# Stage one of a decoder trunk on one Trainium2 core: two weight blocks on each arriving x, another order of transfers, sums and factors at other steps

## The chip, the core and the metric

The kernel runs on one core of one Trainium2 chip. A core has TensorE (matrix products; PE in the profile, with PEld for the loading of its weights), VectorE (DVE), ScalarE (ACT), GpSimd (POOL) and the queue engine SyncE (SP), which here only issues transfers. Products go into PSUM, and everything else lives in SBUF. The metric is the device time of one execution in microseconds, the median over the runs shown.

## The reference, cut to what matters

One layer of a hybrid decoder, T = 1024 tokens and 1024 channels in fp32. The normed input is multiplied by `w_in`, and its columns go to three groups of heads; then come `w_out`, a gated MLP and a gate.

```python
z = rmsnorm(h, norm_mix_g[l]) @ w_in[l]
a_q, a_f, a_i, a_g, b_q, b_k, b_v, c_in = jnp.split(z, splits, axis=-1)
o_a = hgrn2_mix(a_q, a_f, a_i, a_g, ...)
o_b = dilated_window_mix(b_q, b_k, b_v)
o_c, v_first = rwkv7_mix(c_in, ...)
h = h + jnp.concatenate([o_a, o_b, o_c], axis=-1) @ w_out[l]
h = h + conv_glu_ffn(rmsnorm(h, norm_ffn_g[l]), ffn_up[l], ...)
h = h + jax.nn.sigmoid(rmsnorm(h, norm_ple_g[l]) @ ple_gate[l]) * (p[l] @ ple_proj[l])
...
# in rwkv7_mix: a mix of each column with that of the token before
cm = cf + (c_prev - cf) * mu
r, k, v, wd, ad, gd = jnp.split(cm, splits, axis=-1)
w = -jax.nn.softplus(-(w0 + jnp.tanh(wd) @ w2)) - 0.5
a = jax.nn.sigmoid(a0 + ad @ a2)
kk = k * k_k, divided by its norm in each head
state = state * decay + (state @ -kk) (kk a)^T + v k^T      # token by token
```

The factor of the norm, 1 / sqrt(mean(x^2) + eps), is one number for each token.

## The kernel before

x is held transposed: channels on the 128 partitions in 8 tiles k = 0 to 7, tokens along the row in two halves of 512 (HT). A block of `w_in` is 1024 x 128, with index j, brought as one tile of 128 x 1024 (`wraw`) with its 8 pieces side by side. An fp32 product is made of three products of rounded parts (`mm3`, L130, L132, L134): high x by high weight (`whi`), low x (`xl`) by high weight, high x (`xh`) by low weight (`wlo`). For each half of a block (pieces 0 to 3, and 4 to 7) `split2` makes whi by a copy on ACT (L106), and wlo by a subtraction on DVE or POOL (L108). `split_w` chooses the engine by whether a running number is odd; that number counts every tile that gets a name, so it depends on how many were named before.

**Stage one** is `mix_norm` (from L336). The products don't wait for the norm: x is multiplied by its gain g and split into xh (ACT, L378) and xl (DVE, L379), and the factor, called R or rstd, is multiplied in afterwards, on the result. Three blocks of `w_in` are worked on here: j = 0 (in the program later `lora`, the columns wd and ad), j = 1 (`sg`, the column gd) in the pool dps of two PSUM buffers `dp`, and j = 2 (`k`) in `dp2`, which lies in a PSUM pool ps0 that is closed later. Its place then goes to the pool `mx`, from which the small product `lo` (L610) and others take theirs. For the factor, `square` sums x^2 over the tiles (ACT, and the additions on DVE into `acc`); `factor_sums` multiplies by ones on TensorE (L167), scales on DVE (L173) and takes the power on POOL (L175); `factor` spreads the result on TensorE (L181, with the identity in `cst`) and copies it on ACT into R (L395). `idle_products` are products of a constant tile whose result nothing reads (`pwarm`).

The queue of SP brings, in this order: 238 columns of the parameters `par` (119 KB), the halves of w0, x by pairs of tiles, w1, w2, the second half of x, and the constants `cst`; the first two tiles of x come over ACT's queue, the last 512 columns of `par` over POOL's.

**Behind stage one** `rwkv` begins. `mix_in` scales a result with R (`scale`, L308), multiplies by 1 - mu on ACT (L547) and adds mu times the result of the token before on DVE (L548). `rwkv_prep` then makes, from lora, the products `lo` and their sigmoids (`a`, `w`, L611), two exponentials of w (L613, L614), two scans along the tokens on DVE (`gam`, `ig`, L621, each with a tile `dz` that POOL zeroes), and the number `ka`; from k the sums `kks` on TensorE (L634), their power on POOL (`kr`, L638), its widening on ACT (`krw`, L187) and its spread on TensorE (`kkb`); from all that kkn (L652), `ar`, `bhat` (L655), and the copy `bb` (L697), which the product `sc` (L714) takes. Meanwhile TensorE multiplies the blocks r, v and others.

TensorE's order is written out by hand here (`manual_schedule`), and in the first half of stage one also ACT's and DVE's; elsewhere a scheduler orders each engine's instructions by its own estimates.

## Time and profile before

| what | us |
|---|---|
| median of 3 runs (1437.71 to 1438.71) | 1437.77 |
| the profiled execution's own time | 1439.43 |
| its span | 1437.70 |
| TensorE busy | 1412.9 |
| VectorE busy | 1089.5 |
| ScalarE busy | 655.2 |
| GpSimd busy | 452.1 |

The profile shows one execution. A row of its timeline has the start, the length (over all instructions of the row where it has a count behind x), the engine, the line, the operation, what it writes and from what, and in brackets the idle time of the engine ahead of it and what ended that. A row of waits has the waiting instruction, the one that it waited for, the sum, the number and the longest. Matmuls overlap: one of 128 x 512 shows some 0.4 us, and they start 0.23 us apart.

### The profile page before, as it was taken

Reading aid. Unit: us, or ns where it says so; the run is one execution under the profiler, and the core shown is the slowest. Engines: PE = TensorE matmul, PEld = TensorE weight load, DVE = VectorE, ACT = ScalarE, POOL = GpSimd, SP = SyncE. Lnnn points to the kernel's source line nnn. Section 1 sums busy time; section 2 is a strip of 40 time slices with the busy share of each in tenths; the row PEclk is TensorE's granted clock in tenths of the full one; section 3 lists DMA queues with packets and bytes.
Section 4 is the critical chain, followed back from the end, with each engine's and each line's share of the span. In section 5 each row is a group of like instructions: output and inputs, shape, how many; then the busy total and the mean of one; then the engine's idle time right before and its main releaser. Section 6 shows DMA issues by size and latency. Waiting matters only on the chain.

```text
span 1437.7 us, 20276 instructions
## 1 busy us (share of the span) xinstructions
PE 1412.9 (98%) x7406; PEld 1167.0 (81%) x7406; DVE 1089.5 (76%) x1649; ACT 655.2 (46%) x1237; POOL 452.1 (31%) x362
## 2 busy tenths in 40 slices
PE   9999999999999999999999999999999999999997
PEld 7788887888877877788878888888888888888886
DVE  7567575674786787348898988898888799777685
ACT  7531443214535676335644334344444445455552
POOL 2322443124421241222145445454444000001343
PEclk9999999999999999999999999999999999999999
DMA  5223021240350320364423333323333983352344
GB/s 212 76 88 111 30 75 59 83 115 30 104 183 30 118 81 30 99 221 173 166 80 104 110 111 110 105 94 110 103 110 110 326 281 95 101 171 60 117 144 142
DMA packets 80019, 167.84 MB, mean 117 GB/s; under 512 B 20080, under 2 KB 22256, under 8 KB 79920
## 3 DMA queue, kind: packets, MB, share of 16 engines
q1 hardware_dynamic: 66144, 145.97, 31.0%
q10 hardware_dynamic: 12832, 17.04, 3.5%
q0 software_dynamic: 944, 3.54, 0.7%
q8 instruction: 58, 0.95, 0.3%
q14 instruction: 41, 0.34, 0.1%
HBM read 120.12 MB, written 46.40 MB: 116 GB/s over the span
## 4 chain that ended last, share of the span: by engine, by line
PE 86%; DVE 6%; ACT 3%; issue 2%; DMA 1%; POOL 1%; SPq 0%; DVEq 0%; ACTq 0%; POOLq 0%
PE bg L1414 16%; PE bv L1414 12%; PE dp L130 8%; PE dp L132 8%; PE dp L134 8%; PE bg L1732 7%; PE bv L1732 7%; PE hsc L1093 2%; PE bv L130 1%; PE bv L134 1%; PE bv L132 1%; PE swq L1249 1%; PE bg L134 1%; PE bg L130 1%; PE bg L132 1%
## 5 line engine op out<-in xcount | busy, mean ns | idle before, releaser
L130 PE MATMUL dp<-xh,whi 128*128 128x512 f32 x544 | 197.5, 408 | 0.9 <-ACT xh L378 0.8
L132 PE MATMUL dp<-xl,whi 128*128 128x512 f32 x544 | 188.7, 392 | 1.1 <-DVE xl L379 1.1
L134 PE MATMUL dp<-xh,wlo 128*128 128x512 f32 x544 | 188.2, 391 | 0.0
L108 POOL TENSOR_TENSOR wlo<-wraw,whi 128x512 fp32r<-128x512 f32 x63 | 90.4, 1439 | 243.3 <-ACT whi L106 229.3
L108 POOL TENSOR_TENSOR wlo<-raw,whi 128x512 fp32r<-128x512 f32 x84 | 136.4, 1643 | 75.3 <-ACT whi L106 75.3
L1414 PE MATMUL bg<-t,whi 128*128 128x512 f32 x352 | 132.5, 389 | 0.8 <-DVE ct L1617 0.8
L106 ACT CAST whi<-wraw 128x512 fp32r<-128x512 f32 x120 | 72.8, 617 | 120.5 <-PE dp L132 75.8
L130 PEld LDWEIGHTS dp<-xh,whi 128*128 128x128 f32 x544 | 101.8, 189 | 23.8 <-issue 3.4
L134 PEld LDWEIGHTS dp<-xh,wlo 128*128 128x128 f32 x544 | 102.3, 188 | 21.6
L132 PEld LDWEIGHTS dp<-xl,whi 128*128 128x128 f32 x544 | 102.7, 189 | 21.1 <-DVE xl L379 1.7
L108 POOL TENSOR_TENSOR wlo<-s,whi 128x512 fp32r<-128x512 f32 x44 | 66.9, 1521 | 158.2 <-ACT whi L106 155.7
L1732 PE MATMUL bg<-t,whi 128*128 128x512 f32 x308 | 95.0, 389 | 0.0
L1732 PE MATMUL bv<-t,whi 128*128 128x512 f32 x308 | 94.8, 389 | 0.0
L106 ACT CAST whi<-s 128x512 fp32r<-128x512 f32 x66 | 39.1, 621 | 120.7 <-PE bg L1414 113.2
L106 ACT CAST whi<-raw 128x512 fp32r<-128x512 f32 x88 | 52.6, 619 | 90.8 <-issue 48.5
L175 POOL TENSOR_TENSOR rst<-rst,mhalf 128x4 f32<-128x4 f32 (+1 forms) x9 | 10.3, 1140 | 221.4 <-DVE rst L173 221.4
L1414 PEld LDWEIGHTS bg<-t,whi 128*128 128x128 f32 x352 | 66.0, 188 | 14.6 <-ACT whi L106 1.1
L108 DVE TENSOR_TENSOR wlo<-wraw,whi 128x512 fp32r<-128x512 f32 x57 | 45.1, 792 | 38.2 <-ACT whi L106 33.9
L1728 ACT CAST t<-t 128x512 fp32r<-128x512 f32 x77 | 47.8, 622 | 47.5 <-PE bv L1732 33.0
L1732 PEld LDWEIGHTS bv<-t,whi 128*128 128x128 f32 x308 | 57.8, 188 | 12.0
L1732 PEld LDWEIGHTS bg<-t,whi 128*128 128x128 f32 x308 | 57.8, 188 | 12.0
L1414 PE MATMUL bg<-t,wlo 128*128 128x512 f32 x176 | 67.2, 389 | 0.0
(440 smaller groups left out, 3617.4 us busy)
## 6 DMA issues: line engine op xcount, KB each, us to landing
raw<-in_ffn_up_dram SPq DMA_DIRECT2D x44, 512.0 KB, 3.6
wraw<-in_w_in_dram SPq DMA_DIRECT2D x29, 512.0 KB, 3.9
z<-zst SPq DMA_DIRECT2D x18, 512.0 KB, 2.8
gb<-ct SPq DMA_DIRECT2D x33, 256.0 KB, 2.0
t<-gb SPq DMA_DIRECT2D x33, 256.0 KB, 2.8
t<-gt SPq DMA_DIRECT2D x33, 256.0 KB, 2.6
zl<-z SPq DMA_DIRECT2D x16, 512.0 KB, 4.9
wraw<-in_ple_gate_dram SPq DMA_DIRECT2D x16, 512.0 KB, 3.5
```

Source lines behind the costliest of these rows:

```text
L106: nc.scalar.copy(hi, src)
L108: eng.tensor_tensor(lo, src, hi.bitcast(F32), ALU.subtract)
L130: nc.tensor.matmul(ps[hf], wh, xh[hf], start=first, stop=False)
L132: nc.tensor.matmul(ps[hf], wh, xl[hf], start=False, stop=False)
L134: nc.tensor.matmul(ps[hf], wl, xh[hf], start=False, stop=last)
L175: nc.gpsimd.tensor_tensor(r2[:, :n], r[:, :n], self.mhalf[:, :n], ALU.pow)
L1093: nc.tensor.matmul(sc[:, c, :], ks[:, c * P:(c + 1) * P], view(qt, c * P, [2 * n, 64 // n], [HT + n, 2], [1, n]), start=True, stop=True)
L1249: nc.tensor.matmul(pq[h][:, b:b + w], d["q"][hs, qb * P:nk], d["k"][hs, b:b + w], start=True, stop=True)
L1414: nc.tensor.matmul(ps, w[part == 2][:, s], X[k][part == 1], start=start and k == part == 0, stop=k == 3 and part == 2, skip_group_check=no ...
L1728: nc.scalar.copy(xh, x)
L1732: nc.tensor.matmul(ps[m], wt[part == 2][:, m * P:(m + 1) * P], (xh, xl)[part == 1], start=k == part == 0, stop=k == NK - 1 and part == 2)
```

## The change

- Transfers: the 8 columns g of `par` come first, by themselves; then the first halves of w0 and w1, the second pair of x, the second halves of w0 and w1, the other pairs of x, w2, the second half of x, `cst`, and all the rest of `par` on SP's queue (POOL's queue carries none of it now).
- The first whi is made on DVE. The four wlo of blocks 0 and 1 are all POOL's.
- Blocks 0 and 1 are multiplied together for the first half, on each x as it comes. The idle products are 8 and 2 instead of 13 and 4.
- The squares of the first half come behind all of its splits. The sums of the first half move from behind step 2 of block 2 to behind step 5, its factor from behind step 7 of block 2 to behind step 1 of the second half; the second half's sums from behind step 3 to behind step 6, and its factor from behind step 6 to behind step 1 of block 2.
- `mix_in` scales the three early results into an SBUF tile (`zst`), and ACT and DVE read that; before, it scaled them in PSUM, where both read them.
- Since the number of named tiles changes, the engines of wlo swap in each later block of `w_in`, `w_out` and `ple_gate`: the first half's is now DVE's, the second half's POOL's.

At the start of TensorE's queue stood (dp_35 is block 0, xh_17 and xl_18 are k = 0, xh_19 is k = 1)

```order
L373 MATMUL pwarm_163<-warm_161 128x128 x13
L130 MATMUL dp_35_158<-xh_17_105,whi_39_183 128x512
L132 MATMUL dp_35_158<-xl_18_106,whi_39_183 128x512
L134 MATMUL dp_35_158<-xh_17_105,wlo_40_185 128x512
L373 MATMUL pwarm_163<-warm_161 128x128
L130 MATMUL dp_35_158<-xh_19_107,whi_39_183 128x512
```

and now there stands (dp_36 is block 1)

```order
L385 MATMUL pwarm_164<-warm_162 128x128 x8
L401 MATMUL dp_35_159<-xh_17_105,whi_39_179 128x512
L385 MATMUL pwarm_164<-warm_162 128x128 x2
L401 MATMUL dp_35_159<-xl_18_106,whi_39_179 128x512
L401 MATMUL dp_35_159<-xh_19_107,whi_39_179 128x512
L401 MATMUL dp_35_159<-xh_17_105,wlo_40_181 128x512
L401 MATMUL dp_35_159<-xl_20_108,whi_39_179 128x512
L401 MATMUL dp_36_160<-xh_17_105,whi_41_187 128x512
```

The products with a low part of the weight moved behind others that need only whi.

On DVE, around the two scans of `rwkv_prep`, there was this order before (dp_87 is the block r):

```order
L636 TENSOR_SCALAR kr1_101_579<-kks_100_570 128x16
L618 COPY dz_95_544<-w_88_527 128x16
L619 MEMSET w_88_527 128x16
L621 SCALAR_TENSOR_TENSOR gam_96_548<-w_88_527,dz_95_544 128x1024
L618 COPY dz_97_550<-wi_90_529 128x16
L677 COPY gC_135_800<-gam_96_548 128x16
L619 MEMSET wi_90_529 128x16
L621 SCALAR_TENSOR_TENSOR ig_98_554<-wi_90_529,dz_97_550 128x1024
L623 TENSOR_SCALAR ka_99_556<-a_89_528,par_75 128x1024
L308 TENSOR_TENSOR dp_87_508<-dp_87_508,rstd_121 128x1024
L108 TENSOR_TENSOR wlo_152_910<-wraw_146_902,whi_151_908 128x512
L652 SCALAR_TENSOR_TENSOR kkn_114_627<-k_78_486,par_75,kkb_115_628 128x512
```

and there is this one now (dp_90 is the block r):

```order
L667 TENSOR_SCALAR kr1_104_576<-kks_103_567 128x16
L111 TENSOR_TENSOR wlo_152_903<-wraw_149_899,whi_151_901 128x512
L311 TENSOR_TENSOR dp_90_505<-dp_90_505,rstd_121 128x1024
L649 COPY dz_98_541<-w_91_524 128x16
L650 MEMSET w_91_524 128x16
L652 SCALAR_TENSOR_TENSOR gam_99_545<-w_91_524,dz_98_541 128x1024
L649 COPY dz_100_547<-wi_93_526 128x16
L708 COPY gC_138_797<-gam_99_545 128x16
L650 MEMSET wi_93_526 128x16
L652 SCALAR_TENSOR_TENSOR ig_101_551<-wi_93_526,dz_100_547 128x1024
L654 TENSOR_SCALAR ka_102_553<-a_92_525,par_75 128x1024
L683 SCALAR_TENSOR_TENSOR kkn_117_624<-k_81_483,par_75,kkb_118_625 128x512
```

The scaling of r and a wlo went from behind the scans to ahead of them.

On ACT, where the widening of `kr` and the second exponential of w stand, there was this order before:

```order
L613 ACT_TABLE_LOAD
L613 ACTIVATE wi_90_529<-w_88_527 128x1024
L106 CAST whi_148_904<-wraw_146_902 128x512
L614 ACTIVATE w_88_527<-w_88_527 128x1024
L187 COPY krw_103_583<-kr2_102_581 128x512
L187 COPY krw_104_585<-kr2_102_581 128x512
L106 CAST whi_151_908<-wraw_146_902 128x512
```

and there is this one now:

```order
L644 ACT_TABLE_LOAD
L644 ACTIVATE wi_93_526<-w_91_524 128x1024
L190 COPY krw_106_580<-kr2_105_578 128x512
L645 ACTIVATE w_91_524<-w_91_524 128x1024
L190 COPY krw_107_582<-kr2_105_578 128x512
L109 CAST whi_154_905<-wraw_149_899 128x512
```

The first copy moved ahead of the exponential.

```diff
@@ -99,11 +99,14 @@
 
     WB = 6
 
-    def split2(self, src, eng):
+    def split2(self, src, eng, first=None):
 
         nc = self.nc
         hi = self.wpool.tile([P, HT], F32R, tag="whi", name=self.nm("whi"), bufs=self.WB)
-        nc.scalar.copy(hi, src)
+        if first:
+            first.tensor_copy(hi, src)
+        else:
+            nc.scalar.copy(hi, src)
         lo = self.wpool.tile([P, HT], F32R, tag="wlo", name=self.nm("wlo"), bufs=self.WB)
         eng.tensor_tensor(lo, src, hi.bitcast(F32), ALU.subtract)
         return hi, lo
@@ -282,7 +285,7 @@
     def load_params(self):
         nc = self.nc
         nc.sync.dma_start(self.cst, self.a["cst"][:, :NC0])
-        nc.gpsimd.dma_start(self.par[:, PC_LORA:], self.a["par"][:, PC_LORA:])
+        nc.sync.dma_start(self.par[:, PC_MIX + ND:], self.a["par"][:, PC_MIX + ND:])
         nc.gpsimd.tensor_scalar(self.omm, self.par[:, PC_MU:PC_MU + 8], -1.0, 1.0, ALU.mult, ALU.add)
 
     def load_masks(self, tp):
@@ -347,20 +350,29 @@
         with self.tc.tile_pool(name="st", bufs=1) as sp:
             dummy = sp.tile([P, 1], F32, name="dummy")
             nc.scalar.activation(dummy, self.ones, AF.Square)
-            nc.sync.dma_start(self.par[:, :PC_LORA], self.a["par"][:, :PC_LORA])
             xs = [[sp.tile([P, 2, HT], F32, name=f"x{k}_{hf}") for k in range(4)] for hf in (0, 1)]
             xT = self.a["xT"].rearrange("(a two) p t -> a p two t", two=2)
             raws = {j: self.wpool.tile([P, 1024], F32, tag="wraw", name=self.nm("wraw"), bufs=2) for j in (0, 1)}
             raws[2] = sp.tile([P, 1024], F32, name="wraw2")
             for c in (0, 1):
                 nc.scalar.dma_start(xs[0][0][:, c, :], self.a["xT"][c][:, :HT])
-                nc.sync.dma_start(raws[0][:, c * HT:(c + 1) * HT], self.a["w_in"][0][:, c * HT:(c + 1) * HT])
-            for hf, sl in enumerate(halves):
-                for k in range(1 - hf, 4):
-                    nc.sync.dma_start(xs[hf][k], xT[k][:, :, sl])
-                if hf == 0:
-                    for j in (1, 2):
-                        nc.sync.dma_start(raws[j], self.a["w_in"][j])
+            nc.sync.dma_start(g, self.a["par"][:, PC_MIX:PC_MIX + ND])
+
+            def load_x(hf, k):
+                nc.sync.dma_start(xs[hf][k], xT[k][:, :, halves[hf]])
+
+            def load_first(c):
+                for j in (0, 1):
+                    nc.sync.dma_start(raws[j][:, c * HT:(c + 1) * HT], self.a["w_in"][j][:, c * HT:(c + 1) * HT])
+
+            load_first(0)
+            load_x(0, 1)
+            load_first(1)
+            for k in (2, 3):
+                load_x(0, k)
+            nc.sync.dma_start(raws[2], self.a["w_in"][2])
+            for k in range(4):
+                load_x(1, k)
             self.load_params()
             self.early = {j: self.dps.tile([P, T], F32, tag="dp", name=self.nm("dp")) for j in (0, 1)}
             self.early[2] = ps0.tile([P, T], F32, name="dp2")
@@ -384,6 +396,11 @@
                 if k:
                     self.squared = nc.vector.tensor_tensor(acc, acc, t, ALU.add).ins
 
+            def first(j, k, i):
+                wt = w[j](k)[i == 2]
+                nc.tensor.matmul(self.early[j][:, halves[0]], wt, X[k][i == 1][0], start=k == i == 0,
+                                 stop=k == ND - 1 and i == 2)
+
             def product(j, hf, k):
                 self.mm3({hf: self.early[j][:, halves[hf]]}, w[j](k), X[k], k == 0, k == ND - 1, (hf,))
 
@@ -402,42 +419,50 @@
                 parts = []
                 w[j] = lambda k: tuple(t[:, (k % 4) * P:(k % 4 + 1) * P] for t in parts[k // 4])
                 for b, eng in enumerate(engines):
-                    parts.append(self.split2(raws[j][:, b * HT:(b + 1) * HT], eng))
+                    parts.append(self.split2(raws[j][:, b * HT:(b + 1) * HT], eng, nc.vector if j == b == 0 else None))
                     yield
 
             V, G = nc.vector, nc.gpsimd
             with self.tc.manual_schedule(engines={E.PE}):
                 with self.tc.manual_schedule(engines={E.Activation, E.DVE}):
-                    idle_products(13)
-                    w0, w1, w2 = weights(0, V, G), weights(1, V, V), weights(2, V, G)
+                    idle_products(8)
+                    w0, w1, w2 = weights(0, G, G), weights(1, G, G), weights(2, V, G)
                     next(w0)
+                    for k in (0, 1):
+                        split(0, k)
+                    next(w1)
+                    first(0, 0, 0)
+                    idle_products(2)
+                    for jki in ((0, 0, 1), (0, 1, 0), (0, 0, 2), (0, 1, 1), (1, 0, 0), (1, 0, 1), (1, 1, 0), (1, 1, 1),
+                                (0, 1, 2), (1, 0, 2), (1, 1, 2)):
+                        first(*jki)
+                    for k in range(2, ND):
+                        split(0, k)
+                        if k == 3:
+                            next(w0)
+                            next(w1)
+                    for k in range(2, ND):
+                        for i in range(3):
+                            for j in (0, 1):
+                                first(j, k, i)
                     for k in range(ND):
-                        split(0, k)
-                        if k == 0:
-                            next(w0)
-                        product(0, 0, k)
-                        idle_products(1 if k < 4 else 0)
-                    for _ in range(2):
-                        next(w1)
-                    for k in range(ND):
-                        if k in (4, 5):
+                        square(0, k, acc[0])
+                        if k < 2:
                             next(w2)
-                        square(0, k, acc[0])
-                for k in range(ND):
-                    product(1, 0, k)
                 self.dense({0: self.early[2][:, halves[0]]}, w[2], X, ND, halves=(0,),
-                           hooks={2: lambda: r.update(r=factor_sums(acc[0])), 7: lambda: factor(0, r["r"])})
+                           hooks={5: lambda: r.update(r=factor_sums(acc[0]))})
                 for k in range(ND):
                     split(1, k)
                     square(1, k, acc[1])
                 for k in range(ND):
                     for j in (0, 1):
                         product(j, 1, k)
-                    if k == 3:
-                        r1 = factor_sums(acc[1])
+                    if k == 1:
+                        factor(0, r["r"])
                     if k == 6:
-                        factor(1, r1)
-                self.dense({1: self.early[2][:, halves[1]]}, w[2], X, ND, halves=(1,))
+                        r.update(r=factor_sums(acc[1]))
+                self.dense({1: self.early[2][:, halves[1]]}, w[2], X, ND, halves=(1,),
+                           hooks={1: lambda: factor(1, r["r"])})
 
     def project_rest(self, js, hooks={}):
         for j in js:
@@ -541,8 +566,14 @@
 
     def mix_in(self, j, ti, name, slot=None, hooks={}):
         nc = self.nc
+        early = j in self.early
         ps = self.proj(j, hooks)
-        self.scale(ps, self.R)
+        if early:
+            scaled = self.keep.tile([P, T], F32, tag="zst", name=self.nm("zst"), bufs=2)
+            nc.vector.tensor_tensor(scaled, ps, self.R, ALU.mult)
+            ps = scaled
+        else:
+            self.scale(ps, self.R)
         t = (slot or self.slot)(name)
         nc.scalar.activation(t, ps, AF.Copy, scale=self.omm[:, ti:ti + 1])
         nc.vector.scalar_tensor_tensor(t[:, 1:], ps[:, :T - 1], self.par[:, PC_MU + ti:PC_MU + ti + 1],
```

## The prediction

> **What bounds the kernel now.** I read the page first, then the waits of TensorE, then a table by stage, and only then single rows around the first 80 us. The page says how much room there is, the waits say behind whom.
>
> ```profile
> span 1437.7 us, 20276 instructions
> PE 1412.9 (98%) x7406; PEld 1167.0 (81%) x7406; DVE 1089.5 (76%) x1649; ACT 655.2 (46%) x1237; POOL 452.1 (31%) x362
> ...
> PE dp L132 <- DVE xl L379: 1.1, 2, 0.8
> PE lo L610 <- DVE k L548: 0.9, 1, 0.9
> PE sc L714 <- ACT bb L697: 0.8, 3, 0.4
> ...
> 5.00:12.40 7.40, 5.57 (x31) 4.12 (x29) 5.29 (x8) 6.30 (x10) 3.29 (x4) 1.00 1.04 392
> 12.40:27.30 14.90, 14.90 (x74) 12.46 (x73) 14.38 (x22) 13.31 (x25) 2.96 (x2) 1.00 0.66 251
> 76.00:200.00 124.00, 123.75 (x798) 104.71 (x799) 81.43 (x178) 45.56 (x121) 41.82 (x48) 1.00 0.26 79
> ```
>
> TensorE is idle for 1437.7 − 1412.9 = 24.8 us in all, so anything that doesn't take products away can bring at most that. In the table each row has the stretch and its length, then the busy time of PE, PEld, DVE, ACT and POOL, the granted clock, the DMA share and GB/s. TensorE waits while x arrives (5.57 busy of 7.40), 0.9 us before the product `lo`, and hardly at all from 76 to 200 us. So whatever the change brings must come from the start, and it is kept only if no later wait swallows it. The profiled execution took 1439.43 us, 1.73 around its span, which is 1.66 over the median of 1437.77; I work out differences in the profile and take them from the median.
>
> **The change, step by step. First the path of TensorE.**
>
> ```profile
> GB/s 0 0 0 42 62 255 236 382 393 426 393 332 315 402 410 410 401 344 393 414 410 401 434 410 410 406 377 393 385 385 385 393 393 381 389 385 395 381 424 410
> ...
> 1.31 3.92 PE L373 MATMUL pwarm<-warm 128*128 128x128 f32 x19 [1.31 <-DVE few L275]
> 3.60 2.41 PE L373 MATMUL pwarm<-warm 128*128 128x128 f32 x16
> 5.48 0.62 ACT L106 CAST whi<-wraw 128x512 fp32r<-128x512 f32 x1 [2.73 <-DMA wraw<-in_w_in_dram]
> 6.00 0.72 ACT L378 ACTIVATE xh<-x,par 128x512 fp32r<-128x512 f32 x1
> 6.77 0.50 PE L130 MATMUL dp<-xh,whi 128*128 128x512 f32 x1 [0.76 <-ACT xh L378]
> 7.91 1.28 POOL L108 TENSOR_TENSOR wlo<-wraw,whi 128x512 fp32r<-128x512 f32 x1 [3.52 <-ACT whi L106]
> 12.34 0.48 PE L130 MATMUL dp<-xh,whi 128*128 128x512 f32 x1
> 19.70 0.39 PE L134 MATMUL dp<-xh,wlo 128*128 128x512 f32 x1
> ...
> 20.38 0.39 PE L134 MATMUL dp<-xh,wlo 128*128 128x512 f32 x1
> ```
>
> The transfers run at some 0.4 MB per us from 3.5 us on (one figure per half microsecond), so order alone decides what lands when. Ahead of the first product went 119 KB of parameters; now 4 KB of them go first. The first whi and the first xh stood in a row on ACT (5.48, then 6.00); now DVE makes the one beside the other. I estimate w0's first half at 4.6 us, plus one copy of 0.62 to 0.75: first product at 5.25 instead of 6.77 (4.9 to 5.5).
>
> That alone is no gain, since x comes late: the two x of each pair cost 512 KB, 1.3 us. Three L130/L132/L134 products stand 0.68 us apart (19.70 to 20.38), 0.227 each. Before, 12 of the 48 products of blocks 0 and 1 in the first half had been done at 12.34, so 36 × 0.227 = 8.2 brought them to 20.5. Now both blocks are multiplied on each x, 1.36 us for a step k, which is more than a half pair takes to arrive. All four wlo of the two blocks are now POOL's, 1.28 each in a row, the second one at some 9.0; so steps 0 and 1 end at 9.6, x pairs follow at 10.0 and 11.3 by bytes, and 36 products more end at 17.75 (17.0 to 17.9): **2.75 us ahead**, 2.6 to 3.5. The idle products (13 + 4 to 8 + 2) lay in idle time and cost nothing either way. Weight block 2 lands at some 12.6 and is due at 17.75; half 1 of x, last at 18, is due behind block 2, 17.75 + 24 × 0.227 = 23.2 at the earliest; constants and parameters, last at 20, are read first by the first factor, behind that. So the transfers that go back are all covered.
>
> The sums and factors keep their numbers of instructions and change places. A wait of up to 0.4 us can come at the first sums, whose additions now stand beside POOL's last wlo, and I take 0.2. Block 2 of half 1 then ends 2.5 us ahead. The wait of 0.94 at `lo` goes: it waited for DVE's `k` (row 49.00 below) to let go of block 2's PSUM. Now the scaling into SBUF lets go of it, which before ended at 49.00 − 2.19 = 46.8 and will end somewhat earlier. So TensorE gets to `lo` at 50.34 − 0.94 − 2.5 = 46.9: **3.4 us ahead**.
>
> **Second, the path of ACT and DVE**, which does not begin with the products but with the second factor.
>
> ```profile
> 38.52 0.59 ACT L395 COPY rstd<-ps_ss 128x512 f32<-128x512 f32 x1 [5.04 <-PE ps_ss L181]
> 39.29 2.36 DVE L308 TENSOR_TENSOR dp<-dp,rstd 128x1024 f32<-128x1024 f32 x2 [4.59 <-PE dp L134]
> 49.00 1.28 DVE L548 SCALAR_TENSOR_TENSOR k<-dp,par,k 128x1023 f32<-128x1023 f32 x1 [2.19 <-ACT k L547]
> 50.34 1.99 PE L610 MATMUL lo<-lora,par 64*128 64x512 f32 x8 [0.94 <-DVE k L548]
> 52.94 1.26 ACT L611 ACTIVATE w<-lo,par 128x512 f32<-128x512 f32 x2
> 55.12 1.84 PE L634 MATMUL kks<-few,kksq 128*128 128x2 f32 x16
> 56.99 1.05 ACT L614 ACTIVATE w<-w 128x1024 f32<-128x1024 f32 x1
> 57.25 2.90 POOL L638 TENSOR_TENSOR kr<-kr,mhalf 128x16 f32<-128x16 f32 x1 [11.67 <-DVE kr L636]
> 58.52 2.29 DVE L621 TENSOR_TENSOR_SCAN gam<-w,dz 128x1024 f32<-128x1024 f32 x1
> 60.12 1.78 POOL L108 TENSOR_TENSOR wlo<-wraw,whi 128x512 fp32r<-128x512 f32 x1
> 61.84 0.95 POOL L617 MEMSET dz<- 128x1024 f32 x1
> 63.20 2.29 DVE L621 TENSOR_TENSOR_SCAN ig<-wi,dz 128x1024 f32<-128x1024 f32 x1
> 66.05 1.22 DVE L308 TENSOR_TENSOR dp<-dp,rstd 128x1024 f32<-128x1024 f32 x1
> 67.19 0.68 DVE L108 TENSOR_TENSOR wlo<-wraw,whi 128x512 fp32r<-128x512 f32 x1
> 67.79 0.74 DVE L652 SCALAR_TENSOR_TENSOR kkn<-k,par,kkb 128x512 f32<-128x512 f32 x1
> 73.76 1.22 DVE L655 TENSOR_TENSOR bhat<-a,ig 128x1024 f32<-128x1024 f32 x1
> 75.02 1.69 ACT L697 COPY bb<-bhat 64x256 f32<-64x256 f32 x4 [3.78 <-DVE bhat L655]
> 75.91 2.05 PE L714 MATMUL sc<-ar,bb 128*128 128x128 f32 x16 [0.19 <-ACT bb L697]
> ```
>
> The second factor moves from after step 6 of half 1 to after step 1 of block 2, 1.36 + 2 × 0.68 = 2.7 us later in TensorE's order. So TensorE's gain is used up at this place: its end comes at 38.5, as before, and the scaling of the first blocks with it. Every row down to `lo`'s sigmoids hangs on that one; they gain some 0.3 to 1 us (ACT has one whi fewer between, TensorE no longer waits), and end near 53.1 instead of 54.2. Then two exponentials. On ACT the copy of `kr` now stands ahead of the second one and waits for POOL's power, which follows TensorE's `kks`, 3.4 ahead: 57.25 − 3.4 + 2.90 = 56.7. So the second exponential ends at 57.3 to 58.3, against 58.04. On DVE, in the order shown with the change, the scaling of r and a wlo went from behind the scans to ahead of them. The scaling waits for r's last product: kks ended at 55.12 + 1.84 = 57.0, behind it stood the last 18 of r, 4.1 us, so 61.1 − 3.4 = 57.6; it ends at 58.8. So the first scan begins at about 59.1, not 58.52, ends at 61.4; POOL's wlo beside it ends 1.1 us after the scan (60.12 + 1.78 = 61.9 against the scan's end at 60.8), then comes the memset of 0.95, and the second scan begins at 63.9 instead of 63.2. What follows is then shorter by 1.22 + 0.68, less up to 1.1 for a POOL wlo that gets in behind the second scan. kkn comes at 67.5 to 68.7 (before 67.79), and bhat, bb and the product `sc`, in the same order as before, at 74 to 76 (before 75.91). I take 75.0.
>
> The sum: TensorE gains 2.75 at the blocks, loses 0.25 at the sums, gains 0.94 at `lo`, arrives at `sc` at 75.7 − 3.4 = 72.3, and waits there some 2.7 us. It is left with 75.91 − 75.0 = 0.9. Bounds from the same rows: 0 to 1.8. Behind `sc` the order on TensorE is the same, and it stays busy to 200 us, so 0.9 should arrive at the end: 1437.77 − 0.9 = **1436.9**. One thing acts further on: in all later blocks the two wlo swap engines, the first half's now being DVE's. It brings 0.68 instead of 1.28 for the half that is due first, on an engine that is 76% busy instead of 31%: I take 0, bounds −1 and +1.
>
> The Trainium skill's GPSIMD Engine Reference (Specifications) says that GpSimd shares its SBUF interfaces with VectorE and contends with instructions that have two SBUF inputs; the trace agrees, in the wlo beside the scan (1.78 instead of 1.28 us). By that page the change has a cost that I left out: the new scaled tiles make L548's successors read two SBUF inputs, where they read one from PSUM; held by one wlo, such an instruction would be late by up to 1.1 us, and the gain of 0.9 would be −0.2.
>
> **The rivals.** (1) *The gain gets through.* If ACT and DVE run as early as TensorE, `sc` starts at 72.4: −3.5, 1434.3 (−2.9 to −4.5, with a luckier start). For it: the removed 1.9 us ahead of kkn, and POOL's power 3.5 earlier. Against it: the second factor's place, and r's scaling ahead of the scan. It decides if the scans begin before 57.5. (2) *Slower: the swap of the wlo.* If DVE's scans and chains keep first halves waiting in a few later blocks, TensorE waits there: the scan rows are 2.29 us each, two such waits and lesser ones are +3.5, 1441.3. For it: DVE's 76%. Against it: the weights are loaded well ahead, and 123.75 of 124 us busy in the row from 76 shows the depth of that cover. It decides once wlo is late by over a block's lead in two places. (3) *The early products start slow.* The 13 idle products are 26 instructions: the first ten took 1.31 to 3.60, 0.23 apart, the other 16 took 2.41, 0.15. If that quickening comes later after only 8, the first twelve products may stand at twice their spacing: 12 × 0.227 = 2.7, of which 1.1 lie in waits for x, so 1.6 us lost. In the likeliest case that only shortens the wait at `sc`: 1436.9. Only with (1) does it show, 1435.9. Against it: the granted clock column is 1.00 in all rows. The Trainium skill's TensorE: Matmul & The Clock Gate (What's actually happening) says that the array runs at half clock until a window of some 3.4 us has been busy; the spacing of the idle products agrees with it, and by a window that counts time the eight would be enough.
>
> **How the numbers follow.** A measurement of this kernel can tell about 0.2%, 2.9 us, from nothing. Most of the gain lost at `sc`: 0.60, within 0.2%. The gain gets through: 0.25, faster. Slow start: 0.05, within 0.2%. Slower: 0.10. The range goes from 1433.6, near the deep end of rival 1, to 1439.4, the likeliest with both its bounds against it and 0.6 more; it leaves out rival 2 and a thin end of rival 1. The likeliest one's own range is 1435.0 to 1438.8.
>
> **What would show it.** First product (L401) at 5.3; the first half of blocks 0 and 1 ended near 17.75; no wait at `lo`; the second rstd at 38.5; the first scan at 59 behind r's scaling; and a new wait of 2 to 3.5 us at `sc` for `bb`. No wait at `sc` and an end 3 us earlier is rival 1. A prediction that is off by more than that would come from places behind 200 us, which I read as unmoved.

## The result: slower by 0.7%, and the profile after

The changed kernel takes 1447.82 us (median of 6 runs, 1447.18 to 1452.09), the kernel before 1438.36 beside it: a ratio of 1.0072, with a 95% interval of 1.0062 to 1.0082. I had forecast no change that could be told, 1436.9. The profiled execution took 1447.28, its span 1445.6.

The page and the waits of TensorE of the changed kernel, and the row of the table by stage from 76 to 200 us (busy time of PE, PEld, DVE, ACT and POOL, clock, DMA share, GB/s), where TensorE was busy for 123.75 of 124 us before:

```profile
span 1445.6 us, 20252 instructions
PE 1415.3 (98%) x7392; PEld 1166.0 (81%) x7392; DVE 1092.0 (76%) x1647; ACT 654.8 (45%) x1236; POOL 456.3 (32%) x364
...
PE sc L745 <- ACT bb L728: 3.1, 1, 3.1
...
PE bv L170 <- DVE acc L206: 1.6, 1, 1.6
...
PE ps_ss L170 <- DVE acc L206: 1.6, 1, 1.6
...
76.00:200.00 124.00, 119.96 (x765) 101.71 (x766) 82.96 (x174) 43.84 (x116) 38.84 (x46) 1.00 0.26 79
```

The wait at `lo` is gone and the one at `sc` has come, as forecast. But two waits for `acc` have grown to 1.6 us (one was 1.0, the other too short to be listed), far behind stage one, and TensorE is busy for 2.4 us longer although it does seven idle products less. I set the same matmul of both traces side by side and followed the lag of the changed kernel: −0.3 us at `lo` (50 us), +3.2 at `sc` (79), +3.8 at 200, +2.5 at 595, +0.9 at 599, +1.6 at 652, +4.0 at 700, +3.6 at 1350, +6.8 at 1367, +7.9 at the end. So 3.2 us are lost by 79 us, and the rest in short stretches near 655 and 1365.

First, the start and the second factor:

```profile
GB/s 0 0 0 16 150 284 291 385 369 320 303 205 184 213 242 365 393 402 414 410 406 401 426 418 397 381 389 385 389 385 393 385 389 381 393 381 396 401 399 382
...
5.71 0.51 PE L401 MATMUL dp<-xh,whi 128*128 128x512 f32 x1 [0.62 <-DVE whi L107]
9.46 1.34 ACT L390 ACTIVATE xh<-x,par 128x512 fp32r<-128x512 f32 x2 [2.73 <-DMA x<-in_xT_dram]
11.39 2.65 POOL L111 TENSOR_TENSOR wlo<-wraw,whi 128x512 fp32r<-128x512 f32 x2 [2.32 <-ACT whi L109]
12.18 2.07 ACT L390 ACTIVATE xh<-x,par 128x512 fp32r<-128x512 f32 x3 [0.34 <-DMA x<-in_xT_dram]
12.93 1.65 DVE L391 SCALAR_TENSOR_TENSOR xl<-x,par,xh 128x512 fp32r<-128x512 f32 x1 [1.30 <-ACT xh L390]
...
19.76 0.39 PE L133 MATMUL dp<-xh,whi 128*128 128x512 f32 x1
...
27.66 0.15 DVE L176 TENSOR_SCALAR rst<-ps_ss 128x4 f32<-128x4 f32 x1
...
30.02 0.65 PE L184 MATMUL ps_ss<-cst,rst 128*128 128x128 f32 x4 [0.73 <-POOL rst L178]
...
41.95 0.59 ACT L412 COPY rstd<-ps_ss 128x512 f32<-128x512 f32 x1 [1.68 <-PE ps_ss L184]
```

The first product starts at 5.71, not at 5.25. The second pair of x comes at 9.5 and the third at 12.2, not at the 7.5 and 10.0 that the bytes gave; the transfers move some 200 GB/s from 5.5 to 7.5 us where before they moved 300 to 400. Beside POOL's wlo the fifth xl takes 1.65 us instead of 0.74. Block 2 begins at 19.76, not at 17.75: 0.85 us earlier than before, not 2.75. Then DVE scales the first sums only at 27.66, behind its splits, and TensorE waits 0.73 at the first factor. So the second rstd stands at 41.95, not at 38.5.

The chain behind it:

```profile
60.95 1.23 DVE L311 TENSOR_TENSOR dp<-dp,rstd 128x1024 f32<-128x1024 f32 x1 [3.48 <-PE dp L137]
62.46 2.29 DVE L652 TENSOR_TENSOR_SCAN gam<-w,dz 128x1024 f32<-128x1024 f32 x1
...
67.14 2.29 DVE L652 TENSOR_TENSOR_SCAN ig<-wi,dz 128x1024 f32<-128x1024 f32 x1
69.35 1.73 DVE L654 TENSOR_SCALAR ka<-a,par 128x1024 f32<-128x1024 f32 x1
76.89 1.21 DVE L686 TENSOR_TENSOR bhat<-a,ig 128x1024 f32<-128x1024 f32 x1
78.03 1.22 DVE L311 TENSOR_TENSOR dp<-dp,rstd 128x1024 f32<-128x1024 f32 x1
...
82.20 2.12 DVE L711 SCALAR_TENSOR_TENSOR prod<-r,par,k 128x1024 f32<-128x1024 f32 x1
...
63.01 2.83 POOL L111 TENSOR_TENSOR wlo<-wraw,whi 128x512 fp32r<-128x512 f32 x1 [1.86 <-ACT whi L109]
67.56 2.97 POOL L111 TENSOR_TENSOR wlo<-wraw,whi 128x512 fp32r<-128x512 f32 x1 [0.82 <-ACT whi L109]
...
79.07 2.03 PE L745 MATMUL sc<-ar,bb 128*128 128x128 f32 x16 [3.08 <-ACT bb L728]
```

It has the shape that the prediction gave it: r's scaling ahead of the first scan, a POOL wlo beside each scan, held up, the memset behind it, and `ka` held up in turn (1.73 instead of 0.73). It is 4 us later, mostly because it starts later: the first scan begins at 62.46 instead of the forecast 59.1, the second at 67.14 instead of 63.9. The rows at 78.03 and 82.20 are the scaling of v and `prod`, which experiments 2 and 10 come back to.

Last, the two waits for `acc`. The place near 1360, where the sums of the gate's norm are made:

```profile
1355.37 3.99 DVE L206 TENSOR_TENSOR acc<-acc,sqt 128x512 f32<-128x512 f32 x4
...
1356.19 1.82 POOL L111 TENSOR_TENSOR wlo<-wraw,whi 128x512 fp32r<-128x512 f32 x1 [4.61 <-ACT whi L109]
...
1360.61 1.67 POOL L111 TENSOR_TENSOR wlo<-wraw,whi 128x512 fp32r<-128x512 f32 x1 [2.60 <-ACT whi L109]
...
1361.08 2.36 DVE L206 TENSOR_TENSOR acc<-acc,sqt 128x512 f32<-128x512 f32 x2
...
1362.89 1.05 PE L170 MATMUL bv<-few,acc 128*128 128x1 f32 x8 [1.60 <-DVE acc L206]
...
1365.23 0.63 PE L135 MATMUL bv<-xh,whi 128*128 128x512 f32 x1
...
1365.66 0.63 PE L137 MATMUL bv<-xh,wlo 128*128 128x512 f32 x1
...
1364.00:1366.00 2.00, 2.00 (x6) 1.59 (x6) 1.37 (x4) 0.54 (x1) 1.21 (x1) 0.58 0.40 100
1366.00:1368.00 2.00, 2.00 (x6) 1.51 (x5) 0.86 (x2) 0.71 (x2) 0.23 (x1) 0.57 0.81 293
```

and the same place in the kernel before, where TensorE doesn't wait (DVE, POOL, TensorE):

```profile
1350.96 2.23 DVE L203 TENSOR_TENSOR acc<-acc,sqt 128x512 f32<-128x512 f32 x2 [0.27 <-ACT sqt L202]
...
1350.47 1.37 POOL L108 TENSOR_TENSOR wlo<-wraw,whi 128x512 fp32r<-128x512 f32 x1 [4.87 <-ACT whi L106]
...
1357.65 1.05 PE L167 MATMUL bv<-few,acc 128*128 128x1 f32 x8
```

The additions into `acc` take 0.68 us each elsewhere; in the changed kernel four take 3.99 and two 2.36, each group beside a POOL wlo; before, one group of two had a POOL wlo beside it. TensorE waits 1.6 for the last, and 1.4 us behind the wait the granted clock falls: 0.58 and 0.57 over two microseconds each are some 3.4 us at half clock (2 × 2.0 × (0.42 + 0.43)). Products then start 0.43 us apart instead of 0.227, so a stretch costs about 1.6 us. The kernel before has one such stretch in its profiled execution ahead of the very end, behind a wait of 1.68 us for `vt` (0.77 and 0.50 in the rows of 594 to 598); the changed one has two, one near 655 behind the other wait for `acc`, and this one.

That other wait, near 650, is of another kind (changed kernel):

```profile
650.82 0.69 DVE L1560 TENSOR_TENSOR s<-raw,raw 128x512 f32<-128x512 f32 x1 [1.79 <-DMA raw<-in_ffn_up_dram]
651.43 0.68 DVE L206 TENSOR_TENSOR acc<-acc,sqt 128x512 f32<-128x512 f32 x1
...
652.26 1.02 PE L170 MATMUL ps_ss<-few,acc 128*128 128x1 f32 x8 [1.55 <-DVE acc L206]
```

No POOL wlo runs beside this addition, and it takes 0.68. DVE stands idle for 1.79 us until a transfer of the MLP's weight (`raw`) has landed, and the addition stands behind the instruction that waits for it. In the kernel before it is the same, with 2.33 us idle and a wait of 0.99 on TensorE.

### The profile page after: what moved, and what is told of

It is laid out like the page before. It is cut to its first block, busy times and chain, and to the rows that moved or that the text cites. A ratio compares the mean times of both kernels' runs of the same rounds, so it can differ in the third digit from the quotient of the medians.

```text
span 1445.6 us, 20252 instructions
## 1 busy us (share of the span) xinstructions
PE 1415.3 (98%) x7392; PEld 1166.0 (81%) x7392; DVE 1092.0 (76%) x1647; ACT 654.8 (45%) x1236; POOL 456.3 (32%) x364
## 4 chain that ended last, share of the span: by engine, by line
PE 88%; DVE 4%; ACT 2%; issue 2%; POOL 1%; DMA 0%; SPq 0%; DVEq 0%; ACTq 0%; POOLq 0%
PE bg L1445 16%; PE bv L1445 12%; PE dp L133 8%; PE dp L135 8%; PE dp L137 8%; PE bg L1763 7%; PE bv L1763 7%; PE hsc L1124 2%; PE zp L133 1%; PE zp L135 1%; PE swq L1280 1%; PE zp L137 1%; PE bv L133 1%; PE swo L1316 1%; PE bv L135 1%
## 5 line engine op out<-in xcount | busy, mean ns | idle before, releaser
L133 PE MATMUL dp<-xh,whi 128*128 128x512 f32 x528 | 191.3, 409 | 0.3 <-DVE r L579 0.3
L135 PE MATMUL dp<-xl,whi 128*128 128x512 f32 x528 | 182.6, 392 | 0.3 <-DVE xl L160 0.3
L137 PE MATMUL dp<-xh,wlo 128*128 128x512 f32 x528 | 182.0, 392 | 0.0
L111 POOL TENSOR_TENSOR wlo<-wraw,whi 128x512 fp32r<-128x512 f32 x66 | 95.6, 1453 | 249.7 <-ACT whi L109 235.0
L133 PEld LDWEIGHTS dp<-xh,whi 128*128 128x128 f32 x528 | 98.7, 189 | 22.5 <-issue 3.7
L137 PEld LDWEIGHTS dp<-xh,wlo 128*128 128x128 f32 x528 | 99.4, 188 | 21.3
L135 PEld LDWEIGHTS dp<-xl,whi 128*128 128x128 f32 x528 | 99.6, 189 | 19.4 <-DVE xl L160 0.7
```

The source lines that it names most:

```text
L111: eng.tensor_tensor(lo, src, hi.bitcast(F32), ALU.subtract)
L133: nc.tensor.matmul(ps[hf], wh, xh[hf], start=first, stop=False)
L135: nc.tensor.matmul(ps[hf], wh, xl[hf], start=False, stop=False)
L137: nc.tensor.matmul(ps[hf], wl, xh[hf], start=False, stop=last)
```

## The experiments

After the result I had two theories of the loss: the second factor's new place (to 79 us), and the swap of the engines that make wlo in all later blocks. All ratios are against the kernel before, run on the same chip.

**1. The swap undone, in the changed kernel.**

```diff
         self.mix_norm()
+        self.uid += 1
```

> The changed kernel with one thing undone: the running number is raised by one behind stage one, so that in all later blocks the first half's wlo is POOL's again and the second's DVE's, as before the change. Stage one is as changed. Theory (two losses that add: 3.2 us at sc from the second factor's later place, and about 4.7 us behind 200 us from the swapped engines, which end in longer waits for acc and one half-clock stretch more): 1443.1, with sc still waiting about 3 us and the waits of 1.55 and 1.60 us for acc gone or under 1.0. Rival A (all of it comes from stage one, and what stands behind 200 us is its echo): 1447.8, unchanged. Rival B (the half-clock stretches fall by chance, whatever the engines): between 1445 and 1449, with one to three of them in the profile.

Measured: 1440.62, ratio 1.0006 (0.9998 to 1.0014). One number, which chooses nothing but engines, brings back 0.66 of the 0.72%. The wait at `sc` falls to 1.8 and `sc` starts at 76.65; the wait of 1.60 near 1360 is gone, the one near 650 is 1.2, and one half-clock stretch is left. Rival A (all from stage one) falls, and rival B with it (half clock by chance, 1445 to 1449). I had expected 1443.1, so the swap costs more than I read from the one profile.

Of the 3.2 us lost by 79 us, 2.4 go with the swap (76.65 against 79.07). DVE, POOL and TensorE here:

```profile
65.77 2.29 DVE L653 TENSOR_TENSOR_SCAN ig<-wi,dz 128x1024 f32<-128x1024 f32 x1
...
60.47 0.96 POOL L649 MEMSET dz<- 128x1024 f32 x1
...
76.65 2.05 PE L746 MATMUL sc<-ar,bb 128*128 128x128 f32 x16 [1.81 <-ACT bb L729]
```

The memset is done ahead of the first scan, the scaling of r stands between the scans, no POOL wlo runs beside either, and `ka` takes 0.73. So the second scan begins 1.4 us earlier and all behind `ka` 2.4. The swap thus has a hand in the order around the scans; that this order alone is the 2.4 us was not tried.

**2. The swap alone, in the kernel before.** The same line, in the kernel before.

> The kernel before with one thing done: the running number is raised by one behind stage one, so that the engines of wlo swap in all later blocks; everything else is as before. Theory: slower by the second loss alone, about 4 to 5 us, 1443, with the new waits for acc near 650 and 1355. Rival A: 1438.4, unchanged. Rival B: 1437 to 1441, by the number of half-clock stretches only.

Measured: 1446.80, ratio 1.0047 (1.0034 to 1.0061). No part of stage one is changed here, and most of the loss is there. Both waits for `acc` are there, 1.6 us each, and a wait that I hadn't expected: the second group of `sc` waits 2.9 us for `bb`. Rows of DVE, ACT, POOL and TensorE in this kernel:

```profile
75.89 3.50 DVE L681 SCALAR_TENSOR_TENSOR prod<-r,par,k 128x1024 f32<-128x1024 f32 x1
79.31 1.22 DVE L308 TENSOR_TENSOR dp<-dp,rstd 128x1024 f32<-128x1024 f32 x1
...
80.57 1.11 ACT L548 ACTIVATE v<-dp,omm 128x1024 f32<-128x1024 f32 x1 [4.59 <-DVE dp L308]
...
82.09 0.84 ACT L698 COPY bb<-bhat 64x256 f32<-64x256 f32 x2
...
75.94 2.37 POOL L676 TENSOR_TENSOR khat<-k,ig 128x1024 f32<-128x1024 f32 x1 [5.69 <-DVE k L675]
...
82.98 3.39 PE L715 MATMUL sc<-ar,bb 128*128 128x128 f32 x15 [2.89 <-ACT bb L698]
```

and the same products in the kernel before:

```profile
76.64 1.23 DVE L308 TENSOR_TENSOR dp<-dp,rstd 128x1024 f32<-128x1024 f32 x1
77.77 2.02 DVE L680 SCALAR_TENSOR_TENSOR prod<-r,par,k 128x1024 f32<-128x1024 f32 x1
```

With the swap the scheduler puts `prod` ahead of v's scaling. `prod` runs beside POOL's `khat` and takes 3.50 us instead of 2.02; the scaling of v comes 2.7 us later, ACT waits for it, and the copies `bb` stand behind ACT's row on v. Experiment 10 tests this. In the changed kernel itself `prod` stands behind v's scaling (82.20 and 78.03 above), so this order is not what the changed kernel pays at `sc`.

**3 and 4. The second factor at its old place, in the changed kernel; and with the swap undone too.**

```diff
-                    if k == 6:
-                        r.update(r=factor_sums(acc[1]))
-                self.dense({1: self.early[2][:, halves[1]]}, w[2], X, ND, halves=(1,),
-                           hooks={1: lambda: factor(1, r["r"])})
+                    if k == 3:
+                        r1 = factor_sums(acc[1])
+                    if k == 6:
+                        factor(1, r1)
+                self.dense({1: self.early[2][:, halves[1]]}, w[2], X, ND, halves=(1,))
```

> The changed kernel with one thing undone: the second half's sums stand again behind step 3, and its factor behind step 6, of the second half's products; the engines of wlo stay swapped. Theory: the second rstd comes at 39 instead of 41.95, and all that hangs on it moves up; sc waits 0 to 0.7 instead of 3.1: faster by 2.5 to 3.2, 1445.0. Rival C (the scans are late because of the order on DVE and ACT around them, not because of the factor): rstd comes earlier but sc still waits over 2 us, and the time stays over 1447.

Measured: 1447.17, ratio 1.0050 (1.0035 to 1.0065). The first group of `sc` starts 4.7 us earlier, at 74.42, and then the second group waits 2.9 for `bb`, as in experiment 2: what one place gives back, the swap's place takes (`prod` is ahead of v's scaling here, and takes 3.49). By its words, `rstd` earlier but `sc` still waiting over 2 us and a time over 1447, rival C came true; but the wait is another one, at the second group and behind `prod`. The profiled execution, the slowest of six (1449.53, the others from 1444.17), had five half-clock stretches.

> Both undone, the second factor's place and the swap of the engines; transfers, the two blocks at once, the first factor's place and the scaling into SBUF stay. Theory: the two losses add, so 1447.8 - 3 - 4.7 = 1440.1, or by the earlier first product down to 1437.5. Rival A and C: 1445 or more.

Measured: 1438.02, ratio 0.9988 (0.9980 to 0.9997). So what is left of the change is faster than the kernel before, by 0.12%. No wait at `sc` is over 0.4, and TensorE runs 1.0 us ahead from `lo` on, 1.4 from 652 on. From 4 to 1 the factor's new place costs 0.18%, 2.6 us, of which I had forecast the mechanism.

**5 and 6. The swap in parts, in the kernel before:** behind the mixing stage only, and in the mixing stage only.

```diff
                 self.phase_mix()
+                self.uid += 1
```

> The kernel before; the engines of wlo swap only behind the mixing stage, in the blocks of w_out and ple_gate. Theory (the swap costs at three separate places: the second group of sc at 82 us, acc near 650, acc near 1355): the first is absent, the two waits for acc are there (1.6 us each instead of 1.0 and none), and with the half-clock stretch that can follow them it is slower by 2.2 to 4.5: 1441.5 to 1444. Rival D (only the place at 82 counts, the rest is its shift): 1439, no change.

Measured: 1443.90, ratio 1.0026 (1.0015 to 1.0036). The `acc` waits are 1.2 and 1.6, with a half-clock stretch behind each; nothing is lost before 595.

> The kernel before; the engines of wlo swap only in the mixing stage (all w_in blocks behind stage one) and are as before in w_out and ple_gate. Theory: sc's second group waits 2.9 us for bb at 82, the waits for acc are those of before; 3 to 4 slower at 200 us, one given back at 376 (S), so 1441.5 to 1443. Rival D: all of the swap's cost, 1446. Rival B (half-clock stretches by chance): a time that follows their number, with the waits unchanged.

Measured: 1445.04, ratio 1.0032 (1.0021 to 1.0044). The wait of 2.9 at `sc` is there, and the wait near 650 is now 2.3, although the engines are as before in that stage. In its profiled execution half clock lay at 84.6 and, twice as long, at 654.6. That the later wait changed with no edit near it I had not expected. DVE's row there explains its length: it stands idle for 3.61 us until `raw` has landed, 2.33 in the kernel before. Why the transfer lands later against TensorE's work was not tried. The two parts together (0.26 + 0.32) come near the whole (0.47, 0.34 to 0.61).

**7. Scaling in PSUM again,** beside experiment 4.

```diff
-        early = j in self.early
+        early = False
```

> The changed kernel with the second factor's place and the engines of wlo as before, and the three first results scaled in PSUM again. Against the same kernel with the scaling into SBUF (1438.0): Theory: the wait of 0.9 at lo for k comes back, TensorE gets to lo later by it but sc is bound by bb, so the time stays within 0.7: 1438.5. Rival E (the SBUF tiles cost by the shared interfaces): faster, 1437.3 or less.

Measured: 1437.95, ratio 0.9989 (0.9980 to 0.9998): no difference from experiment 4. The line that raises the running number isn't needed here: without the three names of `zst` the engines in the later blocks are those of before, so it is these three names that swap them in the changed kernel. The wait at `lo` didn't come back either, so the scaling into SBUF neither costs nor brings anything that these runs show.

**8. The first factor one step later,** beside experiment 4 (`if k == 2: factor(0, ...)`).

> The changed kernel with the second factor's place and the engines of wlo as before, and the first factor one step later (behind step 2 of the second half instead of step 1). Theory: its wait of 0.6 us for the power goes, the second factor and all that hangs on it move up by that: 1437.4, 0.6 under the kernel with step 1. Rival: the wait at sc takes it back, 1438.0.

Measured: 1439.30, ratio 0.9996 (0.9987 to 1.0005). A miss. Its own wait went, but the second sums now wait 0.55 for DVE, and `sc` waits 0.93. The order that the scheduler gives DVE had changed again.

**9. The second factor's new place alone, in the kernel before** (the edit of experiment 3 the other way).

> The kernel before with one thing done: the second half's sums stand behind step 6 and its factor behind step 1 of block 2 (the changed kernel's place); start, transfers and engines of wlo are as before. Theory: the second rstd comes at 41.2 instead of 38.5, sc waits about 2.7 us for bb in its first group; slower by 2.5, 1441.5. Rival C (the order of ACT and DVE behind it, not the factor): unchanged within 0.7.

Measured: 1440.15, ratio 1.0014 (1.0005 to 1.0023): slower, about by what was expected, but not where. The second rstd comes at 41.17, 2.65 later; TensorE, which is no earlier here, waits 0.5 for `lora` and 1.45 instead of 0.94 at `lo`, and not at `sc`. The lag is 1.2 us from there to 416, where a wait of 1.9 and a half-clock stretch follow.

**10. prod behind the scaling of v,** with the swap in the mixing stage.

```diff
-        nc.vector.scalar_tensor_tensor(prod, r, col(PC_RK), k, ALU.mult, ALU.mult)
+        with tc.issue_after(v_scaled):
+            nc.vector.scalar_tensor_tensor(prod, r, col(PC_RK), k, ALU.mult, ALU.mult)
```

This is the part of the edit that matters; `v_scaled` is the scaling of v, kept when it is issued.

> The kernel before with the engines swapped in the mixing stage alone, as in the run on the swap in that stage, and the product prod kept behind the scaling of v on DVE. Theory (the wait of 2.9 us at the second group of sc comes from prod, 3.5 us beside POOL's khat, getting ahead of v's scaling, on which ACT's copies bb queue): the wait falls from 2.9 to under 0.5 and the kernel gains 2.5 to 3, to 1441.5 to 1442. Rival F (the wait comes from elsewhere in the swap): it stays over 2 us.

Measured: 1437.98, ratio 0.9995 (0.9986 to 1.0004), against 1.0032 without it. DVE and TensorE there:

```profile
74.95 1.22 DVE L309 TENSOR_TENSOR dp<-dp,rstd 128x1024 f32<-128x1024 f32 x1
76.09 2.48 DVE L684 SCALAR_TENSOR_TENSOR prod<-r,par,k 128x1024 f32<-128x1024 f32 x1
...
79.10 2.22 PE L718 MATMUL sc<-ar,bb 128*128 128x128 f32 x16
```

The second group starts at 79.10 instead of 82.57 with no wait. All that the swap in the mixing stage cost the kernel before is gone from the time, by the order of two DVE instructions; the engines are still swapped. So there it isn't the slower or faster wlo that costs, but where the scheduler then puts `prod`. The wait for `acc` near 650 is still there, 1.7 us with a half-clock stretch behind it, and TensorE is 1.7 ahead of the kernel before at 83, which pays for it.

**11. The swap undone in the gate's blocks alone, in the changed kernel** (`self.uid += 1` ahead of `phase_ple`).

> The changed kernel with the engines of wlo as before in the blocks of ple_gate alone. Theory: the wait of 1.6 us for acc near 1360 goes, and with it the half-clock stretch behind it where there is one: faster by 1.6 to 3.2, 1445. Rival: the wait stays, it came from the shift of the stages before; 1447.8.

Measured: 1444.58, ratio 1.0044 (1.0031 to 1.0057), against 1.0072. The wait near 1360 is gone and no half-clock stretch comes there; from 1350 to 1420 the lag doesn't grow, against 3.9 us in the changed kernel. In the changed stretch DVE's additions have one POOL wlo beside them instead of two (DVE, then POOL):

```profile
1355.69 2.23 DVE L206 TENSOR_TENSOR acc<-acc,sqt 128x512 f32<-128x512 f32 x2 [0.27 <-ACT sqt L205]
...
1358.44 1.48 DVE L206 TENSOR_TENSOR acc<-acc,sqt 128x512 f32<-128x512 f32 x2
...
1355.21 1.37 POOL L111 TENSOR_TENSOR wlo<-wraw,whi 128x512 fp32r<-128x512 f32 x1 [4.87 <-ACT whi L109]
```

**12. The second halves' wlo of blocks 0 and 1 on DVE,** beside experiment 4.

```diff
-                    w0, w1, w2 = weights(0, G, G), weights(1, G, G), weights(2, V, G)
+                    w0, w1, w2 = weights(0, G, V), weights(1, G, V), weights(2, V, G)
```

> The changed kernel with the second factor's place and the engines of the later blocks as before, and with the second halves' wlo of blocks 0 and 1 on DVE instead of POOL. Theory (x comes late, and POOL's wlo beside xl add only little): block 2 begins at 19.3 to 19.8 as it did (19.8), the time stays at 1438.0 within 0.5. Rival (POOL's wlo hold DVE's xl up and this made the two blocks late): block 2 begins under 18.8.

Measured: 1437.09, ratio 0.9994 (0.9985 to 1.0003), not told apart from 0.9988. But block 2 begins here at

```profile
18.91 0.39 PE L133 MATMUL dp<-xh,whi 128*128 128x512 f32 x1
```

against 19.84 in experiment 4. So POOL's wlo did hold the two blocks up, by 0.9 us, more than I had expected. The other 1.2 us to the 17.75 of the prediction is what late x leaves. The gain of 0.9 shrinks to 0.2 at the first factor, which waits for POOL's power. Why the transfers fall to 200 GB/s at 5.5 to 7.5 us was not tried.

## Why the prediction was wrong, point by point

- *The swap of wlo: "I take 0, bounds −1 and +1".* This is the step that failed. It costs 0.66% by the ratios of the result and of experiment 1, 9.5 us (the medians, 1447.8 and 1440.6, give 7.2). I weighed it as 0.68 against 1.28 us for a weight part, that is, by whether weights come late. They don't. What it moves is the time at which POOL works beside DVE, and the order that the scheduler makes around it. In the changed kernel that is 2.4 us at `sc`, with a POOL wlo beside each scan (experiment 1 against the changed kernel; which row of that order costs it stays open), and some 3 us near 1360, where the additions into `acc` run beside POOL (experiments 5 and 11). The prediction had read the order around the scans off DVE's queue and had it in its path to `sc`, without seeing that part of it came from the swap. In the kernel before it is `prod` ahead of v's scaling (experiment 10: the whole 0.32% of the mixing stage). What the swap adds at the wait near 650 isn't shown: that wait follows the landing of `raw`, and with the swap undone it is 1.2 against 1.6 with a half-clock stretch behind it all the same.
- *Rival 2 (slower by the swap)* had the cause and the sign, with a chance of 0.10 and a price of 3.5. Its mechanism, first halves waiting on DVE, isn't what the traces show: no product waits for a wlo behind stage one.
- *"2.75 us ahead" at the blocks.* Measured 0.85. The first product came at 5.71, outside the 4.9 to 5.5. Two terms were too small: x's landing, worked out by bytes as if transfers ended one after another, came 2 us later; and DVE's xl were held up by POOL (0.9, experiment 12).
- *The sums and factors.* 0.2 for the first sums was about right; the wait of 0.73 at the first factor wasn't forecast, because I took DVE's scaling of the sums to come as soon as they were there, and DVE's order has it 2.6 us later.
- *"Its end comes at 38.5"* (second factor). It came 3.4 later, mostly by these two (2.0 at the blocks, 0.7 at the first factor). That a later place uses up TensorE's gain was right, and there was hardly any gain to use up: the place alone costs 0.14% to 0.18% (experiments 9, and 1 against 4).
- *No wait at `lo`, a new wait of 2 to 3.5 at `sc`, r's scaling ahead of the scan:* right, 3.1 at `sc`. But `sc` starts at 79.07, not 75.0, so the size of that wait is partly luck: TensorE came to `sc` later than forecast too (76.0, not 72.3). And the reason given for `lo`, the scaling into SBUF, isn't shown: the wait is gone in experiment 7 without it, and in experiment 2 with the swap alone.
- *"Behind `sc` the order is the same, and it stays busy to 200 us, so 0.9 should arrive".* The order of TensorE was the same; the orders of DVE and ACT were not, and 4.7 of the 7.9 us came behind that place.
- *Rival 1 (the gain gets through)* is what experiment 4 shows in small: with the factor's place and the engines as before the rest brings 0.12%.
- *Rival 3 (slow start):* not in the profiled execution of the changed kernel; in that of experiment 3, with the same start, the clock was at half from 8.1 to 11.5 us. Half-clock stretches had their say later, behind the new waits.
- *The Trainium skill's rule on shared interfaces* I used for one place only, and took 1.1 us at most. The Trainium skill's GPSIMD Engine Reference (Specifications) states it for every DVE instruction with two SBUF inputs; the runs agree, `prod` (3.50 and 2.02, both beside POOL, where `k`, of the same form, takes 1.22 in the kernel before with POOL idle) and the additions (3.99 for four instead of four times 0.68) above all.

## What to carry to other kernels

When an edit changes how many names or tiles are made, look for choices that hang on a running number: here one odd number in place of an even one cost 0.66%, and the largest other part that the experiments set apart, the second factor's place, 0.18%. Hold such choices fixed while an edit is timed, and compare the order of every engine that feeds the critical one, not only of that one. Where two engines hold each other up, count pairs that meet, not engine time.

## What the runs showed of the hardware that I had not expected

- A wait of TensorE costs more than its length when a stretch of half clock follows. In the fourteen profiled executions there were none to five of these before the end. Each lasts 3.4 us (once 6.8), with some 1.6 us lost, and began within 2.3 us behind a wait of 1.0 to 2.9 us, or, twice, in the last 0.3 us of a wait of 2.3 and 3.0; but waits of the same length went without: `vt`'s 1.7 us in every kernel, with a stretch behind it in four of the fourteen. The times of one kernel can spread with it: in experiment 3 the three executions of 1449.2 to 1449.5 had a mean granted clock of 0.991 or 0.992, the three of 1444.2 to 1445.2 one of 0.995 or 0.996. That the stretches follow the waits is read from the traces; no run took a wait away and nothing else.
- The Trainium skill's TensorE: Matmul & The Clock Gate (What's actually happening) puts the return to half clock behind an idle window of some 3.4 us. The length of the stretches agrees; the waits ahead of them were shorter than that.
